# A decoder layer on one core: gate products of exact parts, a held prefetch, other PSUM tiles and stores at the end

## The chip, the cores and the metric

One NeuronCore of a Trainium2 chip runs the whole layer in one launch. The metric is the device time in microseconds (us), the median of a few runs. TensorE (PE) does the matmuls, VectorE (DVE), ScalarE (ACT) and GpSimd (POOL) the elementwise work; SyncE (SP) only issues transfers, in the order of its queue.

## The reference, cut to what matters

The input `x` is 256 tokens of 2048 features, `mem` another 256 tokens; everything is float32. With the norms left out:

```python
q, k, v, g_ret, xr, yr, g_a, g_b = split(rmsnorm(h) @ w_in)
ret_out = silu(g_ret) * retention(q, k, v)
xr = causal_dwconv(xr)                                  # 4 taps
xb = xr.reshape(b, s, 16, 128)
gate_r = sigmoid(einsum("bsgi,gij->bsgj", xb, w_a) + b_a)
gate_i = sigmoid(einsum("bsgi,gij->bsgj", xb, w_x) + b_x)
a = exp(-8 * gate_r * softplus(-lam))
hseq = scan(a, sqrt(1 - a * a) * gate_i * xr)           # h_t = a_t h_(t-1) + u_t
rnn_out = gelu(yr) * hseq
h = h + (sigmoid(g_a) * (ret_out @ w_proj_ret) + sigmoid(g_b) * (rnn_out @ w_proj_rnn)) @ w_mix_out
h = h + cross_attention(rmsnorm(h), rmsnorm(mem)) @ w_o
h = h + (silu(conv(rmsnorm(h) @ w_up_gate)) * conv(rmsnorm(h) @ w_up_value)) @ w_down
out = rmsnorm(h) * final_norm_w
```

The two einsums are the gates: 16 groups of 128 features, each with a 128x128 weight for either gate. The FFN is 5632 wide.

## The kernel before, in words

**Exact parts.** PE's fast float32 form keeps fewer bits than float32, so an operand is split into `hi`, a copy in that form, and `lo`, what is left of it. A product is three matmuls: h times hi, l times hi, h times lo (`products_n` L319 for the weight passes, `product` L355 for small operands). Plain float32 matmuls are also to be had; they show as two records each. The gates in `recur` (L685) use these: four of 128x256 for each pair of groups, `sm<-xr,rgw` in the profile.

**The weight stream.** All large weights lie in HBM in the order of use, cut into chunks of four k tiles (1 MB, `raw`, three buffers). `prefetch` (L237) loads the next chunk by SP (L192), ACT copies its two halves of 128x1024 to `hi` (L283, DVE at L281 for the very first) and DVE subtracts `lo` (L284). `chunks` (L296) hands out a chunk after it has prefetched two ahead (`AHEAD`). A chunk is 24 matmuls of 128x512, 5.44 us. Work put off with `later(n, ...)` (L292) is issued n chunks on. `mm` (L221) keeps PE's instructions in the order of the program; a scheduler places the others, save those that are pinned with `keep_in_program_order` or raised with `high_priority`.

**Turning rows.** A product has tokens on partitions; the next pass needs features there. `by_dma` (L364): ACT splits the rows into planes of 16 bits (`pl`, L372, one per token tile), SP issues a transposing transfer for each (`pt<-pl`, L373), and some chunks on ACT joins the planes to `f` (L383). Then `then(f)` goes on, at the residuals with ACT and DVE making the parts `s` (L429, L430) for the next pass.

**The stages** are: q, k, v, g and retention; four recurrence blocks b (L716 to L760), each a pass for xr and one for yr. Behind the xr pass `conv_x` (L722) makes the four taps on ACT and DVE (L727, L729), and three and four chunks later `recur` runs the gates of two pairs of groups and the elementwise recurrence. Behind the yr pass, and four chunks later (three in the last block), `gelu_y` (L744) makes gelu and its parts. Then come the gated merges, the residual behind w_mix_out, memory attention, the residual behind xa_w_o, the FFN in three parts.

**Residual** (L792): for each of four rows of 512 features the product is added to h (L804), then `by_dma`, then the squares for the next norm (L822). The next stage's first pass (w_up behind xa_w_o) reads the rows' parts in order: its chunk 0 needs row 0, chunk 3 row 3. So it may begin while the last row is still being turned.

**The end** (`last_down`, L964): the last 512 features of the down product are made token tile by token tile; for the second tile (tt = 1) in two pieces of 256 features, so that the sum of squares of the first lies beside the second. The pieces lie in the second halves of two PSUM tiles, the first half of one of which holds token tile 0 (L985). DVE adds h (L989) and squares (L991), POOL makes the power (L1000), then each of four 512-feature rows is scaled and stored by a transfer of its own of 256 KB (L1002 to L1012): six by SP and two by ACT's queue, in rows of 2 KB.

**The start:** eight plain warm-up matmuls, two loads of x's transpose around the first piece of weights, and the first four chunks are of two k tiles only (512 KB), the parts of the first two of them made k tile by k tile (L278).

Of the kernel before, what the change touches and what calls it, by code (L numbers as in the profile page):

```python
# [17 lines left out]
P = 128  # L18
D = 2048
S = 256  # L20
# [14 lines left out]
WARM = 8  # L35
# [101 lines left out]
def hybrid_layer(  # L137
# [99 lines left out]
    def prefetch(n):  # L237
        while len(ahead) < n and taken[0] < len(stream):
# [14 lines left out]
            if own:  # L253
                xs.load(k2 + 1)
            for a, b in zip(cuts, cuts[1:]):
                load(raw[:, a:b, :], src[:, a:b, :], early)
                if i == 0 and a == 0:
                    load(*xs.rest, early)
                elif own and a == 0:
                    xs.load(k2 + nk // KH)  # L260
# [12 lines left out]
            for k in range(0, nk, KH):  # L273
# [4 lines left out]
                for cs in (slice(k, k + 1), slice(k + 1, k + 2)) if i < 2 else (slice(k, k + KH),):  # L278
# [17 lines left out]
    def chunks(nk, w, row, c):  # L296
# [4 lines left out]
        for k, n in pieces(i, nk):  # L301
# [3 lines left out]
            prefetch(AHEAD)  # L305
# [58 lines left out]
    def by_dma(rows, then, wait=1):  # L364
# [5 lines left out]
        for tt in range(2):  # L370
            with tc.high_priority(FREE):
                act.copy(planes[:, tt], words[:, tt])  # L372
            sp.dma_start_transpose(  # L373
                out=turned_.rearrange("p h f s -> p (h f) s")[:, :, tt * P : (tt + 1) * P],
                in_=planes[:, tt].rearrange("p h n -> p (h n)"),
            )

# [307 lines left out]
    def recur(b, rgw, xr, pr, aa, tt_, ti):  # L685

        for j in (2 * pr, 2 * pr + 1):
# [3 lines left out]
            for i in range(2):  # L691
                mm(gp[:, i, :], rgw[:, i, j, :], xr[:, j, :], start=True, stop=True)
# [23 lines left out]
    for b in range(4):  # L716
# [3 lines left out]
        xr = {}  # L720

        def conv_x(f, b=b, xr=xr, rgw=rgw):  # L722
# [11 lines left out]
            three = []  # L734

            def both(pr):
                if pr == 0:
                    three.extend(big([P, 4, S], s=n) for n in ("aa", "tt", "ti"))
                recur(b, rgw, xr[0], pr, *three)
# [20 lines left out]
        turned_rows(gemm_n("w_in", 0, xs, NT, O_YR + b * BW), rs0, gelu_y, 4 if b < 3 else 3)  # L760
# [31 lines left out]
    def residual(w, st, out, wcol, steps=None):  # L792
# [3 lines left out]
        for b in range(4):  # L796
# [6 lines left out]
            h = hrow[b]  # L803
            dve.tensor_add(h, h, ended(products[b]))  # L804
            by_dma(h, lambda f, b=b: turn(f, b, out, wcol), 1 + (b == 1))
# [158 lines left out]
    def last_down(b0, hid, n, b):  # L964
# [4 lines left out]
        accs = [acc(), acc()]  # L969
# [8 lines left out]
        for tt in range(2):  # L978
# [4 lines left out]
            for c in range(2):  # L983
                cs = slice(c * S, (c + 1) * S)
                o = accs[c][:, 1, 0:S] if tt else accs[0][:, 0, cs]  # L985
# [9 lines left out]
                if c == 0:  # L995
                    dve.tensor_reduce(out=before, in_=ss3[:, tt, 0:4], axis=AX.X, op=ALU.add)
                    dve.tensor_scalar_add(before, before, EPS * D)
                    pool.tensor_tensor(out=last[:, BW : BW + 1], in0=before, in1=half, op=ALU.pow)  # L998
            r = sp_.tile([P, 1], F32, tag="ro", bufs=5, name=nm("ro"))
            pool.tensor_tensor(out=r, in0=ss3[:, tt, 4:5], in1=mhalf[:, 0:1], op=ALU.pow)  # L1000
            for c in (1, 0, 3, 2):
                y = hrow[c][:, tt, :]  # L1002
                if c == 3:
                    dve.scalar_tensor_tensor(
                        out=y, in0=last[:, 0:BW], scalar=r, in1=wfin[1][:, 1, :], op0=ALU.mult, op1=ALU.mult
                    )
                elif c == 1:
                    dve.tensor_scalar_mul(y, y, r)
                else:
                    act.mul(y, y, r)  # L1010
# [65 lines left out]
```

## Time and profile before

| | us |
|---|---|
| median of 3 runs (2005.92 to 2006.18) | 2006.1 |
| the profiled execution | 2006.16 |
| its span in the trace | 2004.2 |
| PE busy | 1993.6 |
| DVE busy | 1268.9 |
| ACT busy | 1270.2 |
| POOL busy | 8.8 |

The granted TensorE clock over the span is 0.999. Rows of the timeline begin with the start and the duration in us, then engine, line, operation, what is written from what, how many instructions the row stands for, and in brackets the idle time ahead of it and who ended it. SPq and ACTq are the issuing of transfers. In the groups of the page a duration is that of one instruction in ns; a matmul's duration reaches beyond the start of the next one, for matmuls are pipelined: a warm one of 128x512 is followed by the next after 0.23 us. In the view of what an engine waited for, the three figures are the total, the number and the longest. In the table by stretches (windows) the last three columns are granted clock, share of the DMA engines and GB/s.

### The profile page before, as it was taken

What the parts mean: (1) busy time and instruction counts of PE and PEld (TensorE: products, weight loads), DVE (VectorE), ACT (ScalarE), POOL (GpSimd) and SP (SyncE); (2) the same over time, 40 slices, a digit from 0 to 9 for tenths busy, and PEclk for the clock granted to TensorE, in tenths of its full rate; (3) what the DMA queues carried; (4) which work ended last, traced back from release to release, by engine and by line L of the source; (5) the groups of instructions that cost most, each with busy time, mean ns of one, the idle gap of its engine ahead of it and who ended that gap; (6) DMA issues with size and microseconds to landing.
All of it is one profiled execution on the core that took longest, in us unless ns stands there. A gap on an engine that the chain in (4) does not pass through costs nothing.

```text
span 2004.2 us, 23312 instructions
## 1 busy us (share of the span) xinstructions
PE 1993.6 (99%) x8924; PEld 1656.2 (83%) x8924; DVE 1268.9 (63%) x1566; ACT 1270.2 (63%) x1499; POOL 8.8 (0%) x14
## 2 busy tenths in 40 slices
PE   9999999999999999999999999999999999999998
PEld 7888888888888888888888888888888888888887
DVE  6857756888545555566555654667764576754775
ACT  6646548988444555587666666767763577734763
POOL 0000000000000000000000000000000000000000
PEclk9999999999999999999999999999999999999999
DMA  8755657665655556777666567767665577655673
GB/s 328 238 209 172 237 200 206 214 210 179 218 199 192 199 198 212 268 256 241 203 217 211 193 198 206 213 202 226 231 212 194 179 227 229 204 207 202 205 239 119
DMA packets 197904, 425.58 MB, mean 212 GB/s; under 512 B 142240, under 2 KB 146848, under 8 KB 152736
## 3 DMA queue, kind: packets, MB, share of 16 engines
q1 hardware_dynamic: 197360, 423.55, 64.3%
q8 instruction: 70, 1.15, 0.2%
q10 hardware_dynamic: 432, 0.53, 0.1%
q14 instruction: 42, 0.34, 0.0%
HBM read 388.39 MB, written 2.10 MB: 195 GB/s over the span
## 4 chain that ended last, share of the span: by engine, by line
PE 98%; DMA 1%; DVE 0%; ACT 0%; issue 0%; SPq 0%; POOLq 0%; POOL 0%
PE acc L222 96%; PE sm L222 2%; DMA pt<-pl 0%; DMA raw<-in_wall 0%; DVE lo L284 0%; ACT hi L283 0%; SPq L192 0%; ACT pl L372 0%; ACT nat L1010 0%; DVE last L989 0%; DVE nat L804 0%; ACT junk L822 0%; POOLq L1072 0%; POOL last L998 0%; DVE junk L991 0%
## 5 line engine op out<-in xcount | busy, mean ns | idle before, releaser
L222 PE MATMUL acc<-hi,s 128*128 128x512 f32 x5720 | 1757.7, 389 | 1.2 <-DVE last L989 0.8
L222 PEld LDWEIGHTS acc<-hi,s 128*128 128x128 f32 x5720 | 1071.7, 188 | 222.0 <-DVE last L989 1.3
L284 DVE TENSOR_TENSOR lo<-raw,hi 128x1024 fp32r<-128x1024 f32 (+1 forms) x714 | 859.7, 1220 | 596.9 <-ACT hi L283 579.4
L222 PE MATMUL acc<-lo,s 128*128 128x512 f32 x2860 | 1110.0, 388 | 0.5 <-DVE lo L284 0.5
L283 ACT CAST hi<-raw 128x1024 fp32r<-128x1024 f32 (+1 forms) x712 | 734.5, 1050 | 469.4 <-PE acc L222 427.3
L222 PEld LDWEIGHTS acc<-lo,s 128*128 128x128 f32 x2860 | 537.0, 188 | 112.1 <-DVE lo L284 1.3
L383 ACT COPY f<-pt 128x1024 uint16<-128x1024 uint16 x128 | 168.9, 1353 | 99.9 <-DMA pt<-pl 99.9
L372 ACT COPY pl<-rows 128x1024 uint16<-128x1024 uint16 x100 | 99.7, 1045 | 55.2 <-DVE rows L396 42.9
L396 DVE TENSOR_SCALAR rows<-acc,ro 128x512 f32<-128x512 f32 x76 | 53.4, 744 | 6.2 <-PE acc L222 6.2
L917 DVE SCALAR_TENSOR_TENSOR fg<-f,pf,fg 128x255 f32<-128x255 f32 (+1 forms) x88 | 37.4, 479 | 29.7 <-ACT fg L915 29.3
L917 DVE SCALAR_TENSOR_TENSOR fv<-f,pf,fv 128x255 f32<-128x255 f32 (+1 forms) x88 | 36.1, 478 | 3.9 <-ACT fv L915 3.8
L915 ACT ACTIVATE fg<-f,pf 128x256 f32<-128x256 f32 x44 | 22.9, 592 | 0.3
L915 ACT ACTIVATE fv<-f,pf 128x256 f32<-128x256 f32 x44 | 23.1, 592 | 0.0
L729 DVE SCALAR_TENSOR_TENSOR xr<-f,pa,xr 128x255 f32<-128x255 f32 (+2 forms) x48 | 20.2, 480 | 3.4 <-ACT xr L727 3.3
L404 DVE TENSOR_TENSOR s<-f,s 128x512 fp32r<-128x512 f32 x24 | 15.5, 687 | 9.9 <-ACT s L403 9.9
L430 DVE SCALAR_TENSOR_TENSOR s<-f,pb,s 128x256 fp32r<-128x256 f32 x48 | 20.1, 480 | 2.2 <-ACT s L429 2.2
L372 ACT COPY pl<-nat 128x1024 uint16<-128x1024 uint16 x16 | 15.9, 1045 | 7.5 <-DVE nat L804 7.5
L429 ACT ACTIVATE s<-f,pb 128x256 fp32r<-128x256 f32 x48 | 20.6, 503 | 0.0
L222 PEld LDWEIGHTS sm<-s,s 128*128 128x128 f32 x144 | 18.8, 191 | 0.9
L222 PE MATMUL sm<-s,s 128*128 128x256 f32 (+1 forms) x144 | 18.6, 279 | 0.0
L935 ACT ACTIVATE ft<-fg 128x512 f32<-128x512 f32 x22 | 13.9, 632 | 7.3 <-DVE fg L917 7.3
L418 ACT ACTIVATE v<-acc,ro 128x512 fp32r<-128x512 f32 x16 | 11.0, 686 | 10.2 <-DVE v L419 10.2
(137 smaller groups left out, 561.3 us busy)
## 6 DMA issues: line engine op xcount, KB each, us to landing
raw<-in_wall SPq DMA_DIRECT2D x352, 1024.0 KB, 4.9
nat<-in_x SPq DMA_DIRECT2D x8, 512.0 KB, 8.7
raw<-in_wall SPq DMA_DIRECT2D x7, 512.0 KB, 8.6
pt<-pl SPq DMA_TRANSPOSE x128, 3.3
nat<-in_mem SPq DMA_DIRECT2D x4, 512.0 KB, 8.4
xt<-in_x_t SPq DMA_DIRECT2D x3, 512.0 KB, 10.2
xt<-in_mem_t SPq DMA_DIRECT2D x3, 512.0 KB, 4.9
out<-nat SPq DMA_DIRECT2D x6, 256.0 KB, 2.9
```

Of the source, the lines that this page charges most:

```text
L222: tc.keep_in_program_order(pe.matmul(*a, **k))
L283: act.copy(hi[:, ds], raw[:, cs, :])
L284: dve.tensor_tensor(out=lo[:, ds], in0=raw[:, cs, :], in1=hi[:, ds].bitcast(F32), op=ALU.subtract)
L372: act.copy(planes[:, tt], words[:, tt])
L383: act.copy(halves_[:, :, :, cs], turned_[:, :, :, cs])
L396: dve.tensor_scalar_mul(rows[:, tt, :], a[:, tt, :], r[:, tt : tt + 1])
L404: dve.tensor_tensor(out=t[:, :, S:BW], in0=src, in1=t[:, :, 0:S].bitcast(F32), op=ALU.subtract)
L429: act.activation(t[:, j, 0:S], src[:, j, :], AF.Identity, scale=wcol(j))
L430: dve.scalar_tensor_tensor(out=t[:, j, S:BW], in0=src[:, j, :], scalar=wcol(j), in1=t[:, j, 0:S].bitcast(F32), op0=ALU.mult, op1=ALU.subtract,
L729: dve.scalar_tensor_tensor(out=y[:, s:S], in0=z[:, 0 : S - s], scalar=p_cw(3 - s, t), in1=y[:, s:S], op0=ALU.mult, op1=ALU.add,)
L915: act.activation(y, z[:, j, :], AF.Identity, scale=pf[:, 2, t : t + 1], bias=pf[:, 3, t : t + 1])
L917: dve.scalar_tensor_tensor(out=y[:, s:S], in0=z[:, j, 0 : S - s], scalar=pf[:, 2 - s, t : t + 1], in1=y[:, s:S], op0=ALU.mult, op1=ALU.add,)
```

## The change

- The gates become three products of exact parts (twelve matmuls of 128x256 in the place of four plain ones). The weights' parts are made by POOL (a copy and a subtraction of 128x1024 per block, two chunks behind the load), the convolved x's parts by an ACT copy and a DVE subtraction one chunk behind `conv_x`.
- gelu of blocks 0 to 2 is put off by six chunks in the place of four, so it comes behind the next block's convolution.
- In the residual behind xa_w_o (the one without `steps`), row 3 holds the prefetch while its last chunk is worked off. Its transposes are pinned, and then the prefetch goes on, pinned too.
- In `last_down` the two last pieces get PSUM tiles that do not hold token tile 0.
- The final norm's weight is multiplied in before the power is known; the scaled rows go to a buffer of the weight stream, and each token tile is stored by two transfers of 512 KB in rows of 4 KB, both by SP.
- At the start: seven warm-up matmuls; the first piece of weights is loaded ahead of x; the parts of the first four chunks are made k tile by k tile.

```diff
--- before.py
+++ after.py
@@ -32,7 +32,7 @@
 RAW_BUFS = 3
 PART_BUFS = 6
 AHEAD = 2
-WARM = 8
+WARM = 7
 FREE = 300
 RG_WAIT = 3
 EPS = 1e-6
@@ -234,7 +234,9 @@
 
     at = [0]
 
-    def prefetch(n):
+    held = [False]
+
+    def prefetch(n, pin=False):
         while len(ahead) < n and taken[0] < len(stream):
             i = taken[0]
             name, row, nk, c = stream[i]
@@ -250,11 +252,12 @@
             early = i < 2 * len(EARLY)
             own = early and i % 2 == 0
             cuts = range(nk + 1) if i == 0 else range(0, nk + 1, KH) if i < 6 else (0, nk)
-            if own:
+            if own and i > 0:
                 xs.load(k2 + 1)
             for a, b in zip(cuts, cuts[1:]):
-                load(raw[:, a:b, :], src[:, a:b, :], early)
+                load(raw[:, a:b, :], src[:, a:b, :], early or pin)
                 if i == 0 and a == 0:
+                    xs.load(1)
                     load(*xs.rest, early)
                 elif own and a == 0:
                     xs.load(k2 + nk // KH)
@@ -275,7 +278,7 @@
                     xs[k2 + k // KH]
                 hi = wp.tile([P, KH, BW], F32R, tag="hi", bufs=PART_BUFS, name=nm("hi"))
                 lo = wp.tile([P, KH, BW], F32R, tag="lo", bufs=PART_BUFS, name=nm("lo"))
-                for cs in (slice(k, k + 1), slice(k + 1, k + 2)) if i < 2 else (slice(k, k + KH),):
+                for cs in (slice(k, k + 1), slice(k + 1, k + 2)) if i < 4 else (slice(k, k + KH),):
                     ds = slice(cs.start - k, cs.stop - k)
                     if i == 0:
                         dve.tensor_copy(hi[:, ds], raw[:, cs, :])
@@ -302,7 +305,8 @@
             prefetch(1)
             (r_, c_), parts = ahead.pop(0)
             assert (r_, c_) == (row + k * P, c)
-            prefetch(AHEAD)
+            if not held[0]:
+                prefetch(AHEAD)
             yield k, n, parts
             step[0] += 1
             due = [p for p in pending if p[0] <= step[0]]
@@ -361,7 +365,7 @@
 
         return t[:, j, cs], t[:, j, S + cs.start : S + cs.stop]
 
-    def by_dma(rows, then, wait=1):
+    def by_dma(rows, then, wait=1, pin=False):
 
 
         planes = big([P, 2, 2, BW], U16, s="pl")
@@ -370,10 +374,12 @@
         for tt in range(2):
             with tc.high_priority(FREE):
                 act.copy(planes[:, tt], words[:, tt])
-            sp.dma_start_transpose(
+            turning = sp.dma_start_transpose(
                 out=turned_.rearrange("p h f s -> p (h f) s")[:, :, tt * P : (tt + 1) * P],
                 in_=planes[:, tt].rearrange("p h n -> p (h n)"),
             )
+            if pin:
+                tc.keep_in_program_order(turning)
 
         def join():
             f = big([P, 4, S], s="f")
@@ -682,14 +688,23 @@
     K0 = float(np.sqrt(2.0 / np.pi))
     rnn = []
 
-    def recur(b, rgw, xr, pr, aa, tt_, ti):
+    def parts_of(src, copy, minus):
+
+        hi, lo = (big(list(src.shape), F32R, s="rp") for _ in range(2))
+        copy(hi, src)
+        minus.tensor_tensor(out=lo, in0=src, in1=hi.bitcast(F32), op=ALU.subtract)
+        return hi, lo
+
+    def recur(b, wparts, xparts, xr, pr, aa, tt_, ti):
 
         for j in (2 * pr, 2 * pr + 1):
             t = 4 * b + j
             c1 = slice(t, t + 1)
             gp = small()
             for i in range(2):
-                mm(gp[:, i, :], rgw[:, i, j, :], xr[:, j, :], start=True, stop=True)
+                product(
+                    gp[:, i, :], [t[:, i, j, :] for t in wparts], [t[:, j, :] for t in xparts], True, True
+                )
             tr = tp.tile([P, S], F32, tag="tr", bufs=2, name=nm("tr"))
             act.activation(tr, gp[:, 0, :], AF.Tanh, scale=0.5, bias=half_ba[:, c1])
             act.activation(ti[:, j, :], gp[:, 1, :], AF.Tanh, scale=0.5, bias=half_bx[:, c1])
@@ -717,9 +732,10 @@
         rgw = big([P, 2, 4, P], s="rgw")
         for i, src in enumerate((rg_w_a, rg_w_x)):
             sp.dma_start(out=rgw[:, i], in_=src[0, 4 * b : 4 * b + 4].rearrange("g i j -> i g j"))
-        xr = {}
-
-        def conv_x(f, b=b, xr=xr, rgw=rgw):
+        xr, wparts = {}, []
+        later(2, lambda wparts=wparts, rgw=rgw: wparts.extend(parts_of(rgw, pool.tensor_copy, pool)))
+
+        def conv_x(f, b=b, xr=xr, wparts=wparts):
             xr[0] = big([P, 4, S], s="xr")
             for j in range(4):
                 t = 4 * b + j
@@ -731,12 +747,13 @@
                         op0=ALU.mult, op1=ALU.add,
                     )
 
-            three = []
+            three, xparts = [], []
+            later(1, lambda: xparts.extend(parts_of(xr[0], act.copy, dve)))
 
             def both(pr):
                 if pr == 0:
                     three.extend(big([P, 4, S], s=n) for n in ("aa", "tt", "ti"))
-                recur(b, rgw, xr[0], pr, *three)
+                recur(b, wparts, xparts, xr[0], pr, *three)
 
             for pr in range(2):
                 later(RG_WAIT + pr, lambda pr=pr: both(pr))
@@ -757,7 +774,7 @@
                 rnn.append(split_pair(o, 0.5))
 
         turned_rows(gemm_n("w_in", 0, xs, NT, O_XR + b * BW), rs0, conv_x)
-        turned_rows(gemm_n("w_in", 0, xs, NT, O_YR + b * BW), rs0, gelu_y, 4 if b < 3 else 3)
+        turned_rows(gemm_n("w_in", 0, xs, NT, O_YR + b * BW), rs0, gelu_y, 6 if b < 3 else 3)
 
 
     def gated(c0, w, st, b, o):
@@ -801,8 +818,16 @@
                     for _ in range(NT // KC - 1):
                         next(one)
             h = hrow[b]
+            hold = b == 3 and steps is None
+            if hold:
+                for _ in range(NT // KC - 1):
+                    next(products[b])
+            held[0] = hold
             dve.tensor_add(h, h, ended(products[b]))
-            by_dma(h, lambda f, b=b: turn(f, b, out, wcol), 1 + (b == 1))
+            by_dma(h, lambda f, b=b: turn(f, b, out, wcol), 1 + (b == 1), hold)
+            if hold:
+                held[0] = False
+                prefetch(AHEAD, True)
             if b < 2:
                 later(2 + b, lambda h=h, b=b: squares(h, ss, b))
             else:
@@ -966,7 +991,7 @@
         h = hrow[b]
         half = sp_.tile([P, 1], F32, tag="half", bufs=1, name="half")
         dve.memset(half, 0.5)
-        accs = [acc(), acc()]
+        accs = [acc() for _ in range(3)]
         parts = [p for _, _, ps in chunks(n, "ffn_w_down", b0 * BW, b * BW) for p in ps]
 
         def total(o, tt, cs):
@@ -982,7 +1007,7 @@
                 total(accs[0][:, 0, :], tt, slice(0, BW))
             for c in range(2):
                 cs = slice(c * S, (c + 1) * S)
-                o = accs[c][:, 1, 0:S] if tt else accs[0][:, 0, cs]
+                o = accs[1 + c][:, 0, 0:S] if tt else accs[0][:, 0, cs]
                 if tt:
                     total(o, tt, cs)
                 y = last[:, c * S : (c + 1) * S + c]
@@ -996,20 +1021,21 @@
                     dve.tensor_reduce(out=before, in_=ss3[:, tt, 0:4], axis=AX.X, op=ALU.add)
                     dve.tensor_scalar_add(before, before, EPS * D)
                     pool.tensor_tensor(out=last[:, BW : BW + 1], in0=before, in1=half, op=ALU.pow)
+                dve.tensor_tensor(out=last[:, cs], in0=last[:, cs], in1=wfin[1][:, 1, cs], op=ALU.mult)
             r = sp_.tile([P, 1], F32, tag="ro", bufs=5, name=nm("ro"))
             pool.tensor_tensor(out=r, in0=ss3[:, tt, 4:5], in1=mhalf[:, 0:1], op=ALU.pow)
-            for c in (1, 0, 3, 2):
-                y = hrow[c][:, tt, :]
-                if c == 3:
-                    dve.scalar_tensor_tensor(
-                        out=y, in0=last[:, 0:BW], scalar=r, in1=wfin[1][:, 1, :], op0=ALU.mult, op1=ALU.mult
-                    )
-                elif c == 1:
-                    dve.tensor_scalar_mul(y, y, r)
-                else:
-                    act.mul(y, y, r)
-                queue = act if c == 2 else sp
-                queue.dma_start(out=out[0, tt * P : (tt + 1) * P, c * BW : (c + 1) * BW], in_=y)
+            scaled = wp.tile([P, 4, BW], F32, tag="raw", bufs=RAW_BUFS, name=nm("out"))
+            rows = [hrow[c][:, tt, :] for c in range(3)] + [last[:, 0:BW]]
+            for c in range(2):
+                dve.tensor_scalar_mul(scaled[:, 2 * c, :], rows[2 * c], r)
+                late = S if c else 0
+                act.mul(scaled[:, 2 * c + 1, late:], rows[2 * c + 1][:, late:], r)
+                if late:
+                    dve.tensor_scalar_mul(scaled[:, 3, 0:late], rows[3][:, 0:late], r)
+                sp.dma_start(
+                    out=out[0, tt * P : (tt + 1) * P, 2 * c * BW : 2 * (c + 1) * BW],
+                    in_=scaled[:, 2 * c : 2 * c + 2, :].rearrange("p c n -> p (c n)"),
+                )
 
     ss3 = sp_.tile([P, 2, 5], F32, tag="ss3", bufs=1, name="ss3")
 
```

## The prediction

> **What bounds the kernel now.** I read the page's busy times first, then what TensorE (PE) waited for.
>
> ```profile
> PE 1993.6 (99%) x8924; PEld 1656.2 (83%) x8924; DVE 1268.9 (63%) x1566; ACT 1270.2 (63%) x1499; POOL 8.8 (0%) x14
> ```
> ```profile
> PE warm L219 <- DVE half L968: 1.1, 1, 1.1
> PE acc L222 <- DVE last L989: 0.8, 1, 0.8
> PE acc L222 <- DVE lo L284: 0.5, 1, 0.5
> PE acc L222 <- DVE s L430: 0.4, 1, 0.4
> ```
> PE is busy 1993.6 of 2004.2 us, and all its listed waits add up to 2.8 us. So the change can win only at four places: less PE work in the gates, those few waits, the head and the tail. It can lose wherever it makes PE wait anew. All times are of the profiled execution, 2006.16 us; the median of the runs, 2006.1, lies 0.06 below. About 0.2% (4.0 us) is what a measurement here can tell from no change.
>
> **Part 1, the held prefetch (residual behind xa_w_o, row 3).** PE works off w_up chunk by chunk. Before, these rows stand around the place:
>
> ```profile
> 1261.37 0.51 SPq L192 DMA_DIRECT2D raw<-in_wall  x1
> ...
> 1275.63 0.39 PE L222 MATMUL acc<-lo,s 128*128 128x512 f32 x1
> ...
> 1276.70 1.22 DVE L804 TENSOR_TENSOR nat<-nat,acc 128x1024 f32<-128x1024 f32 x1
> ...
> 1277.94 2.00 ACT L372 COPY pl<-nat 128x1024 uint16<-128x1024 uint16 x2 [1.06 <-DVE nat L804]
> ...
> 1279.02 1.25 SPq L373 DMA_TRANSPOSE pt<-pl  x1
> ...
> 1280.36 0.52 SPq L192 DMA_DIRECT2D raw<-in_wall  x1
> ...
> 1280.97 2.16 SPq L373 DMA_TRANSPOSE pt<-pl  x1
> ...
> 1281.09 1.98 ACT L283 CAST hi<-raw 128x1024 fp32r<-128x1024 f32 x2
> ...
> 1281.29 0.61 PE L222 MATMUL acc<-hi,s 128*128 128x512 f32 x2
> ...
> 1282.15 2.36 DVE L284 TENSOR_TENSOR lo<-raw,hi 128x1024 fp32r<-128x1024 f32 x2 [0.57 <-ACT hi L283]
> ...
> 1292.92 0.50 PE L222 MATMUL acc<-hi,s 128*128 128x512 f32 x1 [0.36 <-DVE s L430]
> ```
> Row 3's product ends at 1275.63 + 0.39 = 1276.02. PE then does w_up's chunk 0 and reaches chunk 1 at 1281.29. Chunk 1's weights had been asked for at 1261.37. In the order of the built program SP now issues row 3's two transposes first and only behind them the transfer of chunk 1 (only chunk 0 is already in); the transposes are pinned, and SP's queue is in order. So chunk 1 waits for the product, the add, the plane copies and both transposes:
> add 1276.1 + 1.22 = 1277.3; plane copies 2.00 / 2 each, done at 1278.3 and 1279.3; transposes issued at 1278.4 and 1279.7 (1.25 each). What a transfer does behind two transposes is seen where w_up runs:
>
> ```profile
> 1389.92 3.24 SPq L373 DMA_TRANSPOSE pt<-pl  x2
> 1393.27 1.27 SPq L192 DMA_DIRECT2D raw<-in_wall  x2
> ```
> ```profile
> raw<-in_wall SPq DMA_DIRECT2D x2, 1024.0 KB, 6.4
> ```
> ```profile
> raw<-in_wall SPq DMA_DIRECT2D x1, 1024.0 KB, 7.6
> ```
> ```profile
> raw<-in_wall SPq DMA_DIRECT2D x352, 1024.0 KB, 4.9
> ```
> The transfer is issued right behind the pair, so here at 1281.1. The last column of these DMA rows is the us from issue to landing: 6.4 for the two behind this pair (the second queues behind the first), 7.6 for the one at 1280.36, 4.9 for the median of all. For a transfer with none ahead of it I take 5.4, between the last and the first: landed at 1286.5. Then the first hi (1.98 / 2 = 0.99) and PE restarts at 1287.6 instead of 1281.3: **6.3 us idle**. By 4.9 it is 5.8, by 7.6 it is 8.5. ACT's other work (two squares, two joins, four s) should be done about 1285.9, ahead of the landing.
>
> Behind the restart PE does two matmuls and wants lo, which is ready 1.18 us after hi: 0.75 us more at full clock. And the clock may fall:
>
> ```profile
> 1.05 3.78 PE L219 MATMUL warm<-ones 128*128 128x128 f32 x16 [1.05 <-DVE half L968]
> ...
> 4.73 1.77 PE L222 MATMUL acc<-hi,s 128*128 128x512 f32 x4
> ...
> 6.79 1.07 PE L222 MATMUL acc<-hi,s 128*128 128x512 f32 x4
> ...
> 1996.06 0.28 PE L222 MATMUL acc<-lo,s 128*128 128x256 f32 x1
> ```
> ```profile
> 1996.50:1999.40 2.90, 0.00 (x0) 0.00 (x0) 1.88 (x5) 1.33 (x2) 0.55 (x1) 1.00 0.02 6
> ...
> 1999.50:2004.00 4.50, 0.00 (x0) 0.00 (x0) 0.00 (x0) 0.00 (x0) 0.00 (x0) 0.50 0.65 221
> ```
> The column after the five engines is the granted clock: it is 1.00 until 1999.4 and 0.50 from 1999.5, 3.1 us after the last matmul's end (1996.34). At the start PE is slow (four matmuls in 1.77 us, later in 1.07) until about 6 us, 5 us after its first work at 1.05. [...]
> [...]
>
> What goes: PE's wait for s at 1292.9 (0.36 listed, 0.6 with the pipeline's restart), since the transposes now land early. Part 1: 6.3 + 2.3 - 0.6 = **+8.0** (bounds 5.8 + 0.75 - 0.6 = +5.9, and 8.5 + 2.7 - 0.6 = +10.6). With the transposes landing early there is nothing else to win there, for s was only 0.6 late.
>
> **Part 2, the gates.** Before, eight blocks of four plain matmuls; after, eight blocks of twelve products of exact parts, of the form that the second row shows.
>
> ```profile
> 336.58 1.73 PE sm L222 x8
> ...
> 970.65 2.87 PE sm L222 x24
> ...
> 383.58 1.73 PE sm L222 x8
> ```
> ```profile
> 362.24 1.23 DVE L284 TENSOR_TENSOR lo<-raw,hi 128x1024 fp32r<-128x1024 f32 x1 [1.21 <-ACT hi L283]
> ...
> 377.60 2.55 DVE L729 SCALAR_TENSOR_TENSOR xr<-f,pa,xr 128x255 f32<-128x255 f32 x6 [1.52 <-ACT xr L727]
> ...
> 380.48 2.55 DVE L729 SCALAR_TENSOR_TENSOR xr<-f,pa,xr 128x255 f32<-128x255 f32 x6 [0.33 <-ACT xr L727]
> ...
> 382.95 6.89 DVE L284 TENSOR_TENSOR lo<-raw,hi 128x1024 fp32r<-128x1024 f32 x6
> ```
> Twelve cost 12 x 2.87/24 = 1.44 us against 1.73: 8 x (1.44 - 1.73) = -2.3.
> The parts cost PE nothing if they are ready. The weights' are made on POOL, which is busy 8.8 us in all; a block has 47 us (336.6 to 383.6) and the weights lie there for most of that. No row prices POOL's copy or subtract of 128x1024; even at twice DVE's 1.22 they are ready. x's parts take 1.0 on ACT and 1.2 on DVE per block, and DVE is tight where the second block's first gates stand, at 383.6 (383.0 after two shorter blocks). In the new order DVE has by then done three lo subtractions more (3 x 6.89/6 = 3.45) and the parts' one, and puts off two row copies (1.40); gelu's work moves from ahead of conv to behind it, still ahead of the parts. Counted from DVE's end of conv: 382.95 + 3.45 + 1.2 - 1.4 = 386.2, less the idle times that are then filled (1.2, 1.5 and 0.3 in the brackets): 383.1. One lost start or two make it 0.7 late, all of them 3.1. I take +0.7 once (0 to 3.1); the other blocks have 2 us and more by the same count. Part 2: **-1.6** (-2.3 to +0.8).
>
> **Part 3, start, PSUM tile, stores.**
>
> ```profile
> 11.04 0.70 PE L222 MATMUL acc<-hi,s 128*128 128x512 f32 x2
> ...
> 12.27 0.50 PE L222 MATMUL acc<-lo,s 128*128 128x512 f32 x1 [0.53 <-DVE lo L284]
> ```
> At 12.27 PE comes 0.7 us late (two matmuls of 0.23 from 11.04 with a short stop would end at 11.57), because DVE subtracts lo only when all 128x1024 of hi is there, and then takes 1.2. In halves hi and lo take about half as long, and the first lo is there some 1.1 us sooner: -0.8. One warm-up matmul less and the first weights ahead of x move the first product by at most 0.2, the later loads follow as before: -0.1. Together **-0.9** (-0.3 if the next transfer is then what is late, -1.2 if both count whole).
>
> ```profile
> 1986.22 0.39 PE L222 MATMUL acc<-lo,s 128*128 128x512 f32 x1
> ...
> 1987.45 0.50 PE L222 MATMUL acc<-hi,s 128*128 128x256 f32 x2 [0.84 <-DVE last L989]
> ```
> With a PSUM tile of its own the next product starts one period (0.23) behind 1986.22: 1987.45 - 1986.45 = **-1.0** (-0.84 by the listed wait, to -1.1). The third tile exists, the pool has three.
>
> ```profile
> 1997.99 1.33 ACT L1010 ACTIVATE nat<-nat,ro 128x512 f32<-128x512 f32 x2 [6.62 <-POOL ro L1000]
> ...
> 1998.51 1.30 SPq L1012 DMA_DIRECT2D out<-nat  x3
> ```
> Scaling starts at 1997.99 as before. The first store now needs a DVE and an ACT piece (0.67): issued at 1998.7, 0.2 later; the second after two half pieces and one more, about 1999.2, with its issue done at 1999.5, 0.3 ahead of the last of four. Fewer, larger packets save little: **-0.3** (-0.6 to +0.2).
>
> Sum: 8.0 - 1.6 - 0.9 - 1.0 - 0.3 = +4.2, so 2006.16 + 4.2 = **2010.3 us**. All low ends give +0.5 to all high ends +11, which will not come together; the forecast's own range is 2008.0 to 2012.5.
>
> **Rivals.** (a) *The held transfer costs nothing*: chunk 1 is in time. It has to land by 1280.2, so be issued by 1275, ahead of the product's end. Against it stands the pinned order; for it, that before SP slipped a transfer between the two transposes. Then -0.6 - 1.6 - 0.9 - 1.0 - 0.3 = -4.4: 2001.8, faster. Chance 0.09. (b) *The clock stays full over the gap*: part 1 is 6.3 + 0.75 - 0.6 = 6.5, time 2008.8, within 0.2%. Against it stands the 0.50 above. Chance 0.08. (c) *VectorE is later than counted in the gates*, since its idle starts aren't filled or its subtractions are stretched: the stall is 3.1 instead of 0.7, time 2012.7. DVE between 355 and 391 is where the order leaves least room. Chance 0.13. [...]
>
> **How the numbers follow.** Forecast 0.70, about its middle 2010.3 and 55% of it above 2010.1 (0.39); with (c) slower is 0.52. Within 0.2%: the rest of the forecast and (b), 0.39. Faster: (a), 0.09. The range 2007.0 to 2013.2 leaves out (a), part of (c) and the forecast's tails, 0.2 together.
>
> **What would show it.** PE idle about 6 us at w_up's second chunk, waiting for hi, with the granted clock at 0.50 behind it; the wait for s near 1292 gone; the gates' groups at 1.44 us; no wait for DVE's last; no 0.5 at 12.27; one wait of under 1 us for the parts of the second block. Wrong, if chunk 1's transfer stands ahead of row 3's transposes, if the idle time is under 4 us, or if PE waits for the parts in every block.

## The result: 9 us slower, and the profile after

| | before | after |
|---|---|---|
| median of 5 runs, us | 2006.10 (2005.92 to 2006.25) | 2015.38 (2014.48 to 2017.66) |
| profiled execution, us | 2006.16 | 2014.50 |
| its span, us | 2004.2 | 2012.6 |

The ratio is 1.0047, 95% interval 1.0034 to 1.0060. The direction was forecast, the size was not: +4.2 us predicted, +9.3 by the medians, +8.3 in the profiled execution. One of the eleven runs of `e16` below took 2496 us, in a slow state with a granted clock of 0.75, and is left out of its median. The page and PE's waits of the kernel after, to be held against those of before:

```profile
PE 1994.2 (99%) x8954; PEld 1656.1 (82%) x8954; DVE 1283.8 (64%) x1578; ACT 1270.9 (63%) x1505; POOL 26.2 (1%) x22
```
```profile
PE acc L222 <- ACT hi L286: 5.9, 1, 5.9
PE acc L222 <- DVE s L413: 1.7, 2, 1.1
PE warm L219 <- DVE half L993: 1.1, 1, 1.1
PE acc L222 <- ACT s L435: 1.0, 1, 1.0
PE acc L222 <- ACT s L412: 0.4, 1, 0.4
PE sm L222 <- DVE rp L695: 0.4, 1, 0.4
PE acc L222 <- DVE lo L287: 0.3, 1, 0.3
```
Listed waits were 2.8 us and are 10.8. The first is the held transfer, as forecast. Those on `s` L413 and L412 were not forecast: these are the parts of gelu that w_proj_rnn reads. Nor was the one on `s` L435, 1.0 us at the very start.

Both kernels have 8556 matmuls of 128x512 in the same order, so the n-th of one can be set against the n-th of the other. The difference of their start times is flat except at the places of the table. Before and after are one traced execution each, which matters for the start and for the wait near 1292 (see the experiments).

| place | predicted | measured, profiled executions |
|---|---|---|
| start, up to 12.6 us | -0.9 | -0.23 |
| gates, four blocks | -1.6 | -1.61 (8 x -0.28, and +0.65 in the second block) |
| 504 to 510 us, first reads of `rnn` | 0 | **+3.54** |
| w_up's chunk 1, clock and the wait for s near 1292 | +8.0 | +8.18 |
| PSUM tile | -1.0 | -1.11 |
| behind the last matmul | -0.3 | -0.36 |
| sum | +4.2 | +8.40 |

**The gap.** The timeline of after around w_up's chunk 1, by engines:

```profile
1279.02 2.00 ACT L376 COPY pl<-nat 128x1024 uint16<-128x1024 uint16 x2 [7.69 <-DVE nat L826]
...
1280.10 2.61 SPq L377 DMA_TRANSPOSE pt<-pl  x2
1282.80 11.42 SPq L192 DMA_DIRECT2D raw<-in_wall  x5
...
1282.78 0.39 PE L222 MATMUL acc<-lo,s 128*128 128x512 f32 x1
1289.05 1.22 PE L222 MATMUL acc<-hi,s 128*128 128x512 f32 x2 [5.88 <-ACT hi L286]
...
1287.95 1.99 ACT L286 CAST hi<-raw 128x1024 fp32r<-128x1024 f32 x2 [0.36 <-DMA raw<-in_wall]
```
Transposes, then the transfer at 1282.80, landed by 1287.9 (5.1 us), hi, PE: the chain of the prediction link by link. The granted clock (the third figure from the end) of the same stretch:

```profile
1283.00:1286.40 3.40, 0.17 (x1) 0.00 (x0) 0.00 (x0) 3.06 (x4) 0.43 (x1) 1.00 0.95 276
1286.50:1288.80 2.30, 0.00 (x0) 0.00 (x0) 1.61 (x4) 1.94 (x4) 0.00 (x0) 0.71 0.99 410
1289.00:1294.20 5.20, 5.11 (x11) 3.62 (x12) 4.93 (x5) 4.22 (x5) 0.00 (x0) 0.50 0.91 343
1294.30:1300.00 5.70, 5.70 (x27) 4.70 (x26) 4.41 (x4) 2.61 (x3) 0.00 (x0) 1.00 1.01 423
```
The clock is halved from about 1287.5 (0.29 of 2.3 us is lost, that is 1.3 us at half) to 1294.2, some 6.8 us, of which PE works in 5.2.

**The wait that was not forecast.** PE's rows of after, with the reads of `s` that come late:

```profile
507.79 0.50 PE L222 MATMUL acc<-hi,s 128*128 128x512 f32 x1 [0.52 <-DVE s L413]
...
509.63 0.49 PE L222 MATMUL acc<-hi,s 128*128 128x512 f32 x1 [0.42 <-ACT s L412]
511.27 0.50 PE L222 MATMUL acc<-hi,s 128*128 128x512 f32 x1 [1.14 <-DVE s L413]
```
Followed back, the fourth block's gelu is late because the row copies of its yr pass are late. VectorE's rows, before:

```profile
467.62 1.41 DVE L396 TENSOR_SCALAR rows<-acc,ro 128x512 f32<-128x512 f32 x2
```
and after:

```profile
472.82 0.68 DVE L413 SCALAR_TENSOR_TENSOR s<-rn,s 128x512 fp32r<-128x512 f32 x1
473.42 1.22 DVE L695 TENSOR_TENSOR rp<-xr,rp 128x1024 fp32r<-128x1024 f32 x1
474.56 1.40 DVE L402 TENSOR_SCALAR rows<-acc,ro 128x512 f32<-128x512 f32 x2
```
The copies come 6.9 us later, behind all of the third block's gelu and behind the fourth block's parts (`rp`). Their transposes then meet a transfer in SP's queue, and the second lands 6.4 us after its issue (3.3 is the median of all):

```profile
476.41 1.23 SPq L377 DMA_TRANSPOSE pt<-pl  x1
477.74 0.52 SPq L192 DMA_DIRECT2D raw<-in_wall  x1
478.35 1.23 SPq L377 DMA_TRANSPOSE pt<-pl  x1
```
```profile
478.35 6.43 DMA pt<-pl
```
ScalarE waits for that landing as well, in a step of the fourth block's recurrence that stands ahead of the join of these rows in its order:

```profile
484.87 1.10 ACT L712 ACTIVATE tt<-tr,h 128x256 f32<-128x256 f32 x2 [2.15 <-DMA pt<-pl]
```
The step reads nothing of the transpose; it may wait for a buffer that the transpose still reads, which is not shown. The join comes at 490.21, and gelu and its parts behind it.

### The profile page after: what moved, and what is told of

Same layout as the page of the kernel before. It is cut to its first block, busy times and chain, and to the rows that moved or that the text cites. A ratio compares the mean times of both kernels' runs of the same rounds, so it can differ in the third digit from the quotient of the medians.

```text
span 2012.6 us, 23421 instructions
## 1 busy us (share of the span) xinstructions
PE 1994.2 (99%) x8954; PEld 1656.1 (82%) x8954; DVE 1283.8 (64%) x1578; ACT 1270.9 (63%) x1505; POOL 26.2 (1%) x22
## 4 chain that ended last, share of the span: by engine, by line
PE 94%; ACT 2%; DVE 2%; DMA 1%; issue 1%; POOL 0%; POOLq 0%; SPq 0%; DVEq 0%; ACTq 0%
PE acc L222 93%; PE sm L222 2%; DMA raw<-in_wall 1%; ACT hi L286 1%; DVE lo L287 0%; DMA pt<-pl 0%; ACT f L389 0%; ACT pl L376 0%; DVE xr L745 0%; DVE a L715 0%; ACT tt L712 0%; ACT ti L710 0%; ACT tr L709 0%; DVE s L413 0%; ACT aa L711 0%
## 5 line engine op out<-in xcount | busy, mean ns | idle before, releaser
L435 ACT ACTIVATE s<-f,pb 128x256 fp32r<-128x256 f32 x48 | 20.6, 499 | 0.1
L475 POOL TENSOR_TENSOR ro<-rv,mhalf 128x2 f32<-128x2 f32 (+1 forms) x6 | 6.4, 1070 | 1044.3 <-DVE rv L473 1044.3
```

The lines of the kernel that those rows point to most:

```text
L435: act.activation(t[:, j, 0:S], src[:, j, :], AF.Identity, scale=wcol(j))
```

## The experiments

The theory after the result: the hold costs 8.2 us by SP's order and by the clock; the 3.5 us come from what the change puts ahead of the fourth block's row copies on VectorE. Rivals: gelu's new place, the work of the parts, or GpSimd, does it alone. Each run is set against the median of before on its own chip (2006.2 to 2007.0). On those chips before spreads over 2.2 to 3.2 us and the other kernels over 0.9 to 3.8, so differences below 1 us are read from the traces, matmul against matmul, and not from the medians. A trace is one execution: a step that stands in many of them alike can be trusted, one that stands in a single trace may be chance.

### Taking the parts of the change away

`e1_no_hold`: the changed kernel with

```diff
-            hold = b == 3 and steps is None
+            hold = False
```


> The changed kernel without the held prefetch; all else stays. If the hold costs what the profile of the changed kernel shows (8.2 us from TensorE's idle time at w_up's second chunk, the half clock behind it, less the wait for s that it removes), the profiled execution takes 2014.5 - 8.2 = 2006.3 us, and the runs lie within 0.5 us of each other. If the hold only shows a lateness that would come anyway, it stays above 2010. The wait near 505 to 510 us (3.5 us) is in it by both.

Measured: 2006.34 us (before there 2006.19; ratio 1.0001, 0.9992 to 1.0010). The step at w_up's chunk 1 is gone from the trace, and 3.47 us at 504 to 510 stay. So the hold is 8 of the 9 us. The eleven runs spread over 2.7 us, not 0.5. The wait for s near 1292 is gone **without** the hold too (-0.67), and so it is in every other trace of this document, even in those of `e6` and `e7`, which change the start alone: the hold did not even win that. Near 1280 SP issues the same in `e1`, `e5`, `e6` and `e7` as before, a transpose, a transfer, a transpose, but the second transpose's issue took 2.16 us before (1280.97 in the prediction) and 1.2 us in these. So the wait may have been chance in the one execution of before that was traced; no second trace of before is there to settle it.

`e2_hold_only`: the kernel before with the lines of the hold from the change.

> The kernel before with the held prefetch alone. [...] If hold and gates act on each other, the time is below 2012.

Measured: 2014.55 us, where 2006.1 + 8.2 = 2014.3 was expected, 8.4 above before (ratio 1.0041, 1.0029 to 1.0054); 7.74 in the trace. The hold costs nearly the same alone, so it acts on little else. The 0.4 us less fits the clock: PE works 4.5 us at half clock here and 5.2 in the changed kernel. The five runs spread over 1.2 us, less than before's 27 on that chip (2.5), so the hold does not seem to be what spreads the changed kernel.

`e3_gelu_four` and `e4_gelu_two_only`: the kernel of `e1_no_hold` with gelu put off by 4, 4, 4, 3 and by 6, 6, 4, 3 chunks.

> The changed kernel without the held prefetch, and with gelu at four chunks again in all blocks. Theory: the 3.5 us at 505 to 510 come from the gelu of the third block, which put off stands ahead of the fourth block's row copies on VectorE; then they are gone here: 2006.3 - 3.5 = 2002.8 us, if no new wait appears at the gates. Rival: they come from the parts' own work on ScalarE and VectorE in the fourth block; then they stay, and the time is about 2006.

> The changed kernel without the held prefetch, gelu put off to six chunks in the first two blocks only, four in the third. If the third block's gelu alone is to blame, 2002.8 us as with four in all blocks, and the 0.65 us at the second block's gates decide between the two. By the rival (the parts' work) about 2006.

Measured: 2010.18 and 2006.66 us. The theory of the third block's gelu fell: with gelu at four everywhere PE waits at the gates of three blocks as well, and the wait for `s` remains, 2.3 us in the steps (the waits of `e3_gelu_four`):

```profile
PE sm L222 <- DVE rp L695: 4.1, 3, 1.8
PE acc L222 <- DVE s L413: 1.2, 1, 1.2
```
In `e4_gelu_two_only` it remains as well (1.1 and 0.4 us listed); its traced execution is the slowest of its eleven, 2008.41 us, and has 3.4 us of half clock behind that wait (granted clock 0.57 over 513 to 517 us). Gelu behind the convolution is what lets x's parts be nearly in time.

`e5_gelu_six_only`: the kernel before with

```diff
-rs0, gelu_y, 4 if b < 3 else 3)
+rs0, gelu_y, 6 if b < 3 else 3)
```


> The kernel before with gelu of blocks 0 to 2 put off by six chunks in the place of four, and nothing else. With the run that has the parts and gelu at four, this fills a table of two by two. Theory: the wait near 505 to 510 us comes from what stands ahead of the fourth block's row copies on VectorE; gelu alone puts all of itself but one piece there, so about 1.6 us of the 3.5 stay (3.5 less the parts' 1.2 and a piece of 0.7): 2007.7 us. Rival: it is the parts' work; then no wait is left, and the time is that of before, within 0.3 us.

Measured: 2007.00 us, before there 2007.02 (ratio 1.0000, 0.9992 to 1.0009). No step in its trace between 16 and 1290 us, no wait for L407 (gelu's parts) in its list. The rival wins: gelu's move alone costs nothing, and the wait needs the parts. Its trace also shows that late row copies are not enough by themselves. They come 3.5 us later than before, but the two transposes go out as a pair, and nothing waits:

```profile
471.09 1.41 DVE L396 TENSOR_SCALAR rows<-acc,ro 128x512 f32<-128x512 f32 x2
...
474.07 2.62 SPq L373 DMA_TRANSPOSE pt<-pl  x2
```

### Moving the parts

`e8_parts_later`, from `e1_no_hold`:

```diff
-            later(1, lambda: xparts.extend(parts_of(xr[0], act.copy, dve)))
+            later(2, lambda: xparts.extend(parts_of(xr[0], act.copy, dve)))
```


> The changed kernel without the held prefetch, and with the convolved x's parts one chunk later, so that in the order of the built program the fourth block's row copies stand ahead of these parts and of one piece of gelu. Theory (row copies too late in VectorE's order): the row copies come 1.9 us sooner, and the wait near 505 to 510 us falls from 3.5 to about 1.6; the gates of the blocks may then wait for the parts, up to 1 us each. Median 2004.5 to 2007. Rival (VectorE simply has too much to do): the wait stays at 3 us or more, 2006.3 or above.

Measured: 2008.32 us (before there 2007.02). The wait near 505 is gone in full, not in part, and the fourth block's transposes go out as a pair; but the second block's gates now wait, and the clock is halved behind them (0.90 over 385 to 390 us, 0.70 over 390 to 394; 5.1 us with the gates' gain of 0.56 in it):

```profile
PE sm L222 <- ACT rp L694: 2.6, 1, 2.6
PE sm L222 <- DVE rp L695: 1.0, 1, 1.0
```

`e9_parts_later_in_two`: put off in the third and fourth block only, with before's start, and the parts of four chunks made k tile by k tile. `e12_second_block_gates_later`: put off in the second as well, with its gates one chunk later. `e13_parts_later_in_last`: put off in the fourth only.

In this order their edits of these lines are:

```diff
-            later(1, lambda: xparts.extend(parts_of(xr[0], act.copy, dve)))
+            later(1 if b < 2 else 2, lambda: xparts.extend(parts_of(xr[0], act.copy, dve)))
```
```diff
+            later(2 if b else 1, lambda: xparts.extend(parts_of(xr[0], act.copy, dve)))
...
+                later(RG_WAIT + pr + (b == 1), lambda pr=pr: both(pr))
```
```diff
+            later(1 if b < 3 else 2, lambda: xparts.extend(parts_of(xr[0], act.copy, dve)))
```


> The changed kernel without the held prefetch, with the start of before save that the parts of four chunks are made k tile by k tile, and with the convolved x's parts one chunk later in the third and fourth block only. Summed from the runs so far: gates -1.6 (with 0.65 of waiting in the second block), the wait near 505 to 510 us gone as in the run with all parts later, wait for s near 1292 gone (-0.65), PSUM tile -1.1, stores -0.35, k tile by k tile -0.4 to -1.2: 4.1 to 4.9 us below before. If the third or fourth block now waits at its gates as the second did (5.7 us with the half clock), it is above before.

> As the run with the parts later in the third and fourth block, but also in the second, whose gates are put off by one chunk as well. The second block's parts then have a chunk more: its wait of 0.65 us goes, 0.6 us below that run. If the later recurrence comes too late for the second block's gelu or the third block's parts, a wait shows near 410 to 435 us and it is slower than that run.

> As the run with the parts one chunk later in the third and fourth block, but only in the fourth. Theory: the 3.5 us near 505 to 510 come from the fourth block's own parts, which stand ahead of its row copies on VectorE, not from lateness heaped up in earlier blocks; then they stay away here, and the third block's wait of 1.5 us goes as well: 1.5 us below that run, 4 us below before. Rival: the third block's parts on time make the fourth late again, and 2 us or more of the wait near 505 come back.

Measured: `e9` 2003.92 against 2006.49 (ratio 0.9986, 0.9978 to 0.9995), `e12` 2008.50 against 2006.49, `e13` 2003.79 against 2006.67 (ratio 0.9985, 0.9976 to 0.9993). `e12` missed: the wait moved to the third block's gates, 3.4 and 1.0 us. `e9` still loses 1.5 us there (2.6 us below before, where 4.1 to 4.9 were expected), `e13` no more; it lists 0.5 us of waiting at the fourth block's gates. Its trace ends 4.1 us below before's, but that execution (2002.23) is the fastest of its eleven: by the medians `e13` is 2.9 below before and no better than `e9` beyond the spread, where 1.5 was expected. Its rows of VectorE and SP at the place of the fault:

```profile
470.21 1.41 DVE L401 TENSOR_SCALAR rows<-acc,ro 128x512 f32<-128x512 f32 x2
471.52 0.69 DVE L412 SCALAR_TENSOR_TENSOR s<-rn,s 128x512 fp32r<-128x512 f32 x1
472.12 2.36 DVE L286 TENSOR_TENSOR lo<-raw,hi 128x1024 fp32r<-128x1024 f32 x2
474.78 1.23 DVE L694 TENSOR_TENSOR rp<-xr,rp 128x1024 fp32r<-128x1024 f32 x1 [0.30 <-ACT rp L693]
...
472.88 2.61 SPq L376 DMA_TRANSPOSE pt<-pl  x2
```
The row copies stand ahead of the parts, 4.3 us sooner than in the changed kernel, and the two transposes go out as a pair with no transfer between them. They land 3.2 us after their issue, and ScalarE waits for no landing in the recurrence. So the fourth block's own parts, in the place they had in the order, made the 3.5 us; lateness from earlier blocks did not. The transfer goes with it: every trace with late reads of `s` (the changed kernel, `e1`, `e3`, `e4`, `e15`) has a transfer between these two transposes, and every trace without them has the pair. ScalarE's wait for the landing stands in the changed kernel, `e1` and `e15` (2.1 us each), not in `e3` and `e4`. No run moves the transfer alone, so how the 3.5 us divide between the late copies and the transfer is not shown.

`e15_weights_lo_by_dve` (from `e1_no_hold`) and `e16_last_and_weights_by_dve` (from `e13`):

```diff
-parts_of(rgw, pool.tensor_copy, pool)
+parts_of(rgw, act.copy, dve)
```


> The changed kernel without the held prefetch, with the weights' parts made by ScalarE (copy) and VectorE (subtraction) in the place of GpSimd. In the trace of the changed kernel a VectorE instruction beside GpSimd's subtraction takes 2.2 us more (2.88 in the place of 0.69). Theory A: these stretched instructions make VectorE late in the fourth block; without GpSimd it has 2 to 3 us stretched time less and 1.2 us of work more per block, and the 3.5 us near 505 to 510 shrink by 1 us or more: 2005.3 or less against 2006.3 without the hold. Theory B: they fall where VectorE has room; the wait stays at 3.5, and the time at 2006.3 or above.

> The same change of engine on the run with the parts one chunk later in the fourth block only (2.9 us below before there). By theory A its last wait at the gates (0.5 us at the fourth block) goes, and it is 0.5 us below that run; by theory B it is the same within 0.5 us, or slower if ScalarE is now late.

Measured: 2006.92 and 2006.15 us, before there 2006.90 (ratios 1.0000, 0.9991 to 1.0009, and 0.9996, 0.9987 to 1.0005). At 504 to 510 `e15` loses 3.66 us. Theory A falls: GpSimd is not the cause, though VectorE is slower beside it (2.88 us for 0.68, below). `e16` is slower than `e13` in its trace: the fourth block's gates wait for their parts (1.7 us), and the mean granted clock is 0.998 (0.999 in `e13`).

### The hold's price

`e10_hold_behind_two`, from `e9`, with the hold and in it

```diff
-            dve.tensor_add(h, h, ended(products[b]))
+            last = ended(products[b])
+            if hold:
+                prefetch(AHEAD + 1, True)
+            dve.tensor_add(h, h, last)
```


> The same with the pinned transposes of row 3, but the transfers of w_up's chunks 1 and 2 pinned ahead of them. If the hold's price is the order of transfer and transposes in SP's queue alone, the same time as the run without any hold, within 0.5 us. If pinned transposes cost in another way (the join, the scheduler's order), 2 us or more above it.

Measured: 2004.16 us against 2003.92 for `e9` on the same chip, no step at 1281 in the trace. Its rows of SP:

```profile
1279.00 1.25 SPq L376 DMA_TRANSPOSE pt<-pl  x1
1280.34 0.52 SPq L192 DMA_DIRECT2D raw<-in_wall  x1
1280.95 1.24 SPq L376 DMA_TRANSPOSE pt<-pl  x1
```
Pinned transposes cost nothing. But the order is that of `e9`: chunks 1 to 4 are issued ahead of the transposes (the last at 1275.46), and a transfer stands between them, for only the first two are pinned and the scheduler places the others. So no prefetch is held here at all. The run fits that the late transfer is what costs; it does not show a hold in force that is free.

`e11_hold_filled` and `e14_hold_filled_longer`: `e2_hold_only` with 22 and with 29 matmuls of ones behind w_up's chunk 0 (`steps_n`):

```diff
+            if w == "ffn_w_up" and k0 == 0 and not filled:
+                filled.append(1)
+                fill = small()
+                for _ in range(22):
+                    mm(fill[:, 0, 0:P], ones, ones, start=True, stop=True)
```


> The kernel before with the held prefetch, and with 22 matmuls of ones (their result is not read) behind w_up's chunk 0, which keep TensorE busy for most of the gap. If about 2 us of the hold's 8.4 are the half clock behind the gap, the granted clock stays at 1.00 there and the time is 2 us below the run with the hold alone: 6.2 to 6.6 us above before. If the clock has no part in it, 8.4 above before, or more.

> The kernel before with the held prefetch and 29 matmuls of ones in the gap (22 left 1.7 us idle, and the clock was halved for 3.4 us all the same). [...] If the clock falls again, or the fill reaches past hi, no gain.

Measured: 8.1 and 7.0 us above before (2014.57 against 2006.49, 2013.65 against 2006.67), where about 6.5 was expected of the second. The first was inconclusive: it left PE 1.7 and 0.5 us idle, and the clock fell for some 3.4 us:

```profile
1287.90 0.73 PE L222 MATMUL acc<-hi,s 128*128 128x512 f32 x2 [1.67 <-ACT hi L285]
1289.16 0.74 PE L222 MATMUL acc<-lo,s 128*128 128x512 f32 x1 [0.53 <-DVE lo L286]
```
```profile
1287.00:1290.00 3.00, 1.57 (x4) 1.04 (x5) 2.12 (x2) 2.50 (x3) 0.00 (x0) 0.88 1.01 423
1290.00:1294.00 4.00, 4.00 (x13) 3.11 (x13) 3.78 (x5) 3.29 (x4) 0.00 (x0) 0.67 0.87 289
```
The second leaves no gap ahead of hi, and the clock stays:

```profile
1281.90:1288.20 6.30, 6.30 (x58) 6.30 (x57) 1.79 (x5) 5.48 (x8) 0.48 (x1) 1.00 0.99 343
1288.20:1292.00 3.80, 3.38 (x16) 2.50 (x15) 3.66 (x4) 2.83 (x3) 0.00 (x0) 1.00 0.88 330
```
Its step in the trace is 6.56 us where `e2` has 7.74, 1.2 us less (1.4 by the medians). PE's restart in `e2` and in `e14`:

```profile
1287.40 1.22 PE L222 MATMUL acc<-hi,s 128*128 128x512 f32 x2 [5.83 <-ACT hi L285]
```
```profile
1288.25 0.71 PE L222 MATMUL acc<-hi,s 128*128 128x512 f32 x2
```
The product ends 0.45 us later in the trace of `e14`, the restart 0.85, for its transfer landed 0.3 us later. So the gap itself is 0.4 us longer there (6.4 in the place of 6.0). Without the 0.67 that every trace gains near 1292 the two steps are 8.4 and 7.2, so what is lost behind the restart falls from 2.4 to 0.8 us: the half clock costs 1.6 us of the hold in `e2`, the wait for lo 0.8, and the rest is the late transfer.

### The start

`e6_start_only` is before with the change's three edits of the start, `e7_halves_only` with one of them:

```diff
-slice(k + 1, k + 2)) if i < 2 else
+slice(k + 1, k + 2)) if i < 4 else
```


> The kernel before with the three edits at the start alone (seven warm-up matmuls, first weights ahead of x, the parts of four chunks k tile by k tile). By the prediction -0.9 us. By the changed kernel's trace the first product starts 0.6 us later and 0.8 us are won at the third chunk: -0.2 us. If the later first product costs more when the clock rises later, it is slower by 0.3 to 0.8 us.

> The kernel before with only the parts of the first four chunks made k tile by k tile. By the prediction's reading this is the part of the start that wins: -0.8 us, and the first product starts as before at 4.7 us. If the next transfer is late anyway, 0.

Measured: 2006.67 and 2005.83 against 2007.02 (ratios 0.9998, 0.9989 to 1.0007, and 0.9994, 0.9986 to 1.0003). Neither is clear of the spread; the two differ by 0.8 in the sense that the other two edits cost. The traces, matmul against matmul behind the start, say the same. With the change's start they stand 0.6 to 1.2 us later than before's trace in six runs and 0.24 us earlier in the changed kernel itself (0.7 later in the mean of the seven); with before's start they stand at -0.1 to +0.6 (four runs), with the k tiles alone at -0.5 to +0.6 (six, 0.1 in the mean). So the k tiles alone win nothing that shows, the other two edits cost some 0.6 us, and the -0.23 of the table was the luckiest start of seven. The trace of the changed kernel shows how they cost:

```profile
4.77 0.91 ACT L435 ACTIVATE s<-xt,pa 128x256 fp32r<-128x256 f32 x2 [2.02 <-DMA xt<-in_x_t]
5.33 1.63 PE L222 MATMUL acc<-hi,s 128*128 128x512 f32 x4 [1.03 <-ACT s L435]
```
With the weights first, x lands last; `s` begins at 4.77 where it began at 3.22, and the first product at 5.33 where it began at 4.73. In all seven traces `s` begins at 4.4 to 4.8 (3.1 to 3.6 with before's order of loads) and the first product waits for it. The starts differ in another way too: the trace's first record of a granted clock of 1.00 begins 6.0 us after the start in before and 4.0 us after it in the changed kernel.

## Why the prediction was wrong in size, point by point

- **Part 1 held** (8.0 said, 8.2 measured): raw behind the transposes, 5.1 us to land where 5.4 was taken, PE 6.0 us late, the half clock, all as written. "What goes: PE's wait for s" was credited to the hold; `e1_no_hold` shows that it goes without it, so this 0.6 came true by luck and the hold's own price is 8.2 + 0.6 (8.6 said). The 2.3 in its sum stands for the wait for lo and the half clock together; no run shows that term, and no row of before how long the clock stays halved. In its place `e2` and `e14` together give 0.8 for lo and 1.6 for the clock. The stretches at half clock were about 6.8 us in the changed kernel and 3.4 us in `e11`.
- **Part 2 failed at one step**: "puts off two row copies (1.40)" and "the other blocks have 2 us and more by the same count". The gates' own sum was right (-1.61 measured, -1.6 said; the second block's 0.65, 0.7 said), and the other blocks' gates do not wait. But the count asked only when the *parts* are ready for the gates. Row copies that are put off were booked as time won, and their own readers at nothing. In the fourth block these are the two transposes, the join, the last gelu and then w_proj_rnn, some 33 us from the copies to the first late read (474.56 to 507.79), at the only block whose gelu is read at once. In place of 0 the runs showed 3.5 us, which go when the fourth block's parts stand behind the copies (`e8`, `e9`, `e13`). Rival (c) named a congestion of VectorE, but at 355 to 391 and not here.
- **Part 3**: the PSUM tile (-1.1) and the stores (-0.36) held. The start did not: "One warm-up matmul less and the first weights ahead of x move the first product by at most 0.2" was wrong. It moved by 0.6 in this trace and by 0.3 to 0.6 in the seven, because it then waits for x's own path (landing, ACT, PE). That made -0.23 in place of -0.9 here, and +0.7 in the mean of the seven traces.
- The rest of the distance, 0.9 us between the profiled execution and the median of the five runs, is spread of the changed kernel's runs (2014.48 to 2017.66). Its cause is not settled: neither the hold alone nor the changed kernel without the hold spreads more than before does on the other chips. Two things fit: the traced execution had the best start of seven, and two of the three slower runs list a lower mean clock (0.996, where the two fastest list 0.997 and 0.998).
- Rivals (a) and (b) fell with the rows above. The range ended at 2013.2, just above rival (c) with its one congested block (2012.7). All low ends of the terms add up to +0.7 and all high ends to +10.5, not to the +0.5 and +11 said; nothing rests on that.

## What to carry to other kernels

A piece of work that is put off or added may cost nothing at its own reader; what it costs is behind its new place, so list what its engine does next there and follow that to its reader, in the block with the shortest way to one. Look at the queue of transfers on that way too: the same late copies cost nothing as long as no transfer came between their transposes. A prefetch that is held back for a transpose pays the whole way of the transfer (here 5 us of landing and 1 of conversion) if no chunk more is already in; that a chunk more would make such a hold free is not shown here. And a short wait of TensorE that is seen in one execution is worth a second trace before a change is built on it: the one that the hold was to remove stood in no other trace.

## What the runs showed of the hardware

In the changed kernel VectorE's instructions took longer beside GpSimd's subtraction. Of these rows the first and the third lie beside it, the second does not:

```profile
394.64 2.88 DVE L719 SCALAR_TENSOR_TENSOR ti<-ti,xr 128x512 f32<-128x512 f32 x1
442.99 0.68 DVE L719 SCALAR_TENSOR_TENSOR ti<-ti,xr 128x512 f32<-128x512 f32 x1
437.66 5.41 DVE L287 TENSOR_TENSOR lo<-raw,hi 128x1024 fp32r<-128x1024 f32 x2
```
```profile
393.73 3.25 POOL L695 TENSOR_TENSOR rp<-rgw,rp 128x1024 fp32r<-128x1024 f32 x1
438.72 3.26 POOL L695 TENSOR_TENSOR rp<-rgw,rp 128x1024 fp32r<-128x1024 f32 x1
```
A VectorE instruction of 0.68 us took 2.88, and two subtractions that take 2.36 elsewhere took 5.41: 2 to 3 us per block, about as long as GpSimd's own 2.4 to 3.3. In `e15`, where GpSimd makes no parts, L719 takes 0.68 or 0.69 us each time. It cost the kernel nothing here: without it the time is the same (`e15`). Why VectorE's instructions are longer beside GpSimd's is not shown.

In `e8`, `e11` and `e12` the granted clock fell to 0.5 behind waits of 0.5 to 3.4 us. In `e11` PE stood still for 1.67 us up to 1287.90, worked 0.73, waited 0.53, and the fall came at about 1289.3. In `e8` and `e12` waits of 2.6 and 3.4 us at the gates, each with one of 1.0 behind it, were each followed by 3.4 us of granted clock 0.5, which is 1.7 us lost (`e8`: 0.90 over 5 us and 0.70 over 4; `e12`: 0.90 over 6 us and 0.81 over 6). In `e16`, with two waits of 0.8 and 0.9 us at the gates, the mean granted clock of the execution is 0.998; in `e13`, with one of 0.5, it is 0.999.
